# A split-fp32 decoder layer on one core: where the weights' low parts are made, which tile two copies use, and when the second half's sigmoids run

## The chip, the cores and the metric

One NeuronCore of a Trainium2 chip runs the kernel. The metric is the device time of one execution in microseconds (us); of the kernel before, three timed runs and one profiled execution are given. Its engines are TensorE (PE in the profile; PEld is its loading of weights), VectorE (DVE), ScalarE (ACT), GpSimd (POOL) and SyncE (SP), which here issues nearly all DMAs.

## The reference

One decoder layer on x of 2048 rows by 1024 columns, float32:

```python
xn = rms_norm(x, ln_g)
b, c, xc, gc, xl, gl = split(xn @ w_in)            # 6 parts of 1024 columns
y_conv = b * conv3(c * xc)                         # causal, depthwise
u = conv4(xl) + lru_conv_b
r, i = sigmoid(u @ w_a + b_a), sigmoid(u @ w_i + b_i)   # 16 heads of 64
a = exp(8 * r * log_sigmoid(lam))
h[t] = a[t] * h[t-1] + sqrt(1 - a[t]**2) * i[t] * u[t]
y = [headnorm(y_conv) * silu(gc), headnorm(h) * silu(gl)]
out = rms_norm(x + y @ w_out, final_g)
```

Two large products (1024 by 6144, and 2048 by 1024) make nearly all of the work on TensorE.

## The kernel before

**Products.** Each float32 operand is split into a high part (a cast to the matmul's float32r type, on ScalarE) and a low part (the operand minus the high part). A product is three matmuls: high with high, high with low, low with high (`mm`, line 924 of the profile). Seven products instead of eight per 2x2 block arrangement (Strassen's scheme in Winograd's form) are used, so sums of blocks are formed first (`add`) and results are added behind (`put`).

**Steps.** The work goes in steps of one block column. In the first half of the rows (h = 0) and in the second half (h = 1) three steps make a round: l (the LRU's input and its gate), a (two inputs of the short convolution) and b (its third input and its gate). Then come 16 steps o for the output projection. A step has seven slots; in each, twelve matmuls of 128x512 go into one PSUM bank. The order of the products is 0, 6 (of the step before), 1, 3, 2, 4, 5. Products 0, 1 and 2 of a step add up in one bank, called A; after each of them ScalarE copies the bank's state out: `q1` (line 1229) at slot 0, `u2` (line 1232) at slot 2, `rr` (line 1235) at slot 4. The next product into A may start only when the copy before it is done. `q1`, `u2` and `rr` have one tile each. `put(22)` reads rr in the same step; `put(21)` reads u2 at slot 1 of the next step, when product 6 is done (`pend`). Both are additions on VectorE (line 163, as all additions, subtractions and products of two tensors).

**Weights.** In the first half, `s_plan` splits the weights for step n+1 during step n and a little of n+1: `hi(i)` is the cast on ScalarE (line 200), `lo(i)` the subtraction. From step 4 to 23, lo(0), lo(4) and lo(6) run on GpSimd, the other four on VectorE. Each tile holds a high and a low part, and there are seven tiles in all (`sp`), so a cast must wait until PE has read the tile's last content and until its store has landed: the split weights are stored to DRAM (`sd`, line 205) two slots after the low part, or three where GpSimd made it. The second half loads them from there.

**What is due later.** `at(k, f)` puts f off by k slots and `tick()` runs what is due at the start of each slot; this sets the order of instructions on every engine. So the LRU's work runs over the two steps behind its own: the high and low parts of u (`sth`, `stl`; tile st) 5 and 6 slots after product 5, `gates(0)` (four matmuls into two gate banks, line 704) at 8, `sigs(0)` (their four sigmoids on ScalarE, line 711) at 9, `gates(1)` at 10 into the same two banks, `sigs(1)` at 11, then the decay, the scan and the rest up to 17. `silu` multiplies a gate by its sigmoid on GpSimd (tiles gl and gb).

Of the kernel before, what the change touches and what calls it, by code (L numbers as in the profile page):

```python
# [12 lines left out]
F32 = mybir.dt.float32  # L13
# [10 lines left out]
KT = D // P  # L24
# [14 lines left out]
def hymba_kernel(ctx: ExitStack, tc: tile.TileContext, x, xt, w_in, par, lamc, w_gate, w_out, final_g, out):  # L39
    nc = tc.nc  # L40
# [103 lines left out]
    def at(slots, *fs):  # L144
        if slots == 0:
            for f in fs:
                f()
        else:
            due.append([slots, fs])
# [20 lines left out]
    def low(v, hl, eng=None):  # L170
        tt(hl[1], v, hl[0].bitcast(F32), ALU.subtract, eng)
# [7 lines left out]
    def s_plan(n, r, dst):  # L179
        a11, a12, a21, a22 = r  # L180
        t, tiles = {}, {}

        def add(i):
            if i == 2:
                t[2] = aux("s1")
                tt(t[2], a21, a22, ALU.add)
            elif i == 1:
                t[1] = aux("s2")
                tt(t[1], t[2], a11, ALU.subtract)
            elif i == 3:  # L190
                tt(a21, a11, a21, ALU.subtract)
            else:
                tt(t[1], a12, t[1], ALU.subtract)

        def val(i):
            return {0: a11, 1: t.get(1), 2: t.get(2), 3: a21, 4: a12, 5: t.get(1), 6: a22}[i]

        def hi(i):
            tiles[i] = s_tile(dst, i)
            nc.scalar.copy(dst[i][0], val(i))  # L200

        def lo(i, eng=None):
            low(val(i), dst[i], eng)
            if PLAIN <= n < 3 * KT:
                at(3 if eng else 2, lambda: nc.sync.dma_start(sd[n][i], tiles[i].bitcast(F32)))

        g = nc.gpsimd if PLAIN < n < 3 * KT else None
        return [lambda: (add(2), add(1)),
                lambda: (hi(0), lo(0, g), add(3)),
                lambda: hi(1),  # L210
                lambda: (hi(3), lo(1)),
                lambda: (hi(2), lo(3), add(5)),
                lambda: (hi(4), lo(4, g), lo(2)),
                lambda: hi(5),
                lambda: (hi(6), lo(6, g), lo(5))]


    PLAIN = 3
# [18 lines left out]
    class TPrep:  # L237
# [12 lines left out]
        def lo(self, i, eng=None, v=None):  # L250
            low(self.val(i) if v is None else v, self.dst[i, self.j], eng)
# [410 lines left out]
    def lru(h, k, late=0):  # L662
# [33 lines left out]
        def gates(i):  # L696
            sl = slice(i * C, (i + 1) * C)
            if i == 0:
                v["r"], v["i"] = wt("r", "r"), wt("ig", "i", bufs=IG)
            v["ps"] = ps = []  # L700
            for j in range(2):
                ps.append(pss.tile([P, C], F32, tag="s", name="gate"))
                for n in range(2):
                    nc.tensor.matmul(ps[j], v["gw"][n][:, j, :], v["st"][j][:, sl],  # L704
                                     start=(n == 0), stop=(n == 1))

        def sigs(i):
            sl = slice(i * C, (i + 1) * C)
            for j, (hi, lo) in enumerate(((LO, HI), (HI, LO))):
                for g_, src, bias in ((v["r"], hi, BA), (v["i"], lo, BI)):  # L710
                    nc.scalar.activation(out=g_[hi, sl], in_=v["ps"][j][src], func=AF.Sigmoid,  # L711
                                         bias=pt[src, bias + k:bias + k + 1])
# [36 lines left out]
        def put(which, bank, other):  # L749
            dst = {11: o1[:, 4:4 + C], 12: o1[:, 4 + C:4 + N2], 21: g[:, 0:C], 22: g[:, C:N2]}[which]  # L750
            combine(dst, bank, other)
            if which == 12:
                at(1, c0)
                at(2, lambda: cj(1), lambda: cj(2), keep, gw)
                at(3, lambda: cj(3))
                for slots, *fs in ((5, sth), (6, stl), (8, lambda: gates(0)), (9, lambda: sigs(0)),
                                   (10, lambda: gates(1)), (11, lambda: sigs(1)), (12, s1, s0),
                                   (13, s1b), (14, s2, s3), (15, s4), (16, s5), (17, out_)):
                    at(slots + late, *fs)
            if which == 21:  # L760
                silu(g, late)
# [170 lines left out]
    def sm(tag):  # L932
        return small.tile([P, C], F32, tag=tag, name=tag)
# [29 lines left out]
    with tc.manual_schedule(engines={ENG.PE, ENG.Activation, ENG.DVE, ENG.Pool, ENG.SP}):  # L963
# [182 lines left out]
        for n in range(PLAIN, N):  # L1146
# [29 lines left out]
            for s in range(6 if late else 8 if new or last else 7):  # L1176
# [50 lines left out]
                if i == 0:  # L1227
                    q1 = sm("q1")
                    nc.scalar.copy(q1, bk["A"])  # L1229
                elif i == 1:  # L1230
                    u2 = sm_u2[0] = sm("u2")
                    nc.scalar.copy(u2, bk["A"])  # L1232
                elif i == 2:
                    rr = sm("rr")
                    nc.scalar.copy(rr, bk["A"])  # L1235
                    put(22, bk["B"], rr)
                    if late:
                        put(12, bk["D"], rr)
                elif i == 4:
                    put(11, bk["C"], q1)  # L1240
                elif i == 5 and not late:
                    put(12, bk["A"], None)
                elif i == 6:
                    put(21, bk["B"], u2)
# [50 lines left out]
```

## Time and profile before

| | us |
|---|---|
| median of three runs | 1357.18 (1356.16 to 1359.64) |
| the profiled execution | 1361.65 |
| its span | 1359.8 |
| PE / DVE / ACT / POOL busy | 1301.9 / 1032.5 / 748.4 / 226.2 |
| one round of the first half, steady | 60.70 |

The span is the time from the first to the last instruction of the profiled execution. In a row of the groups stand the line, engine, operation, the tile written and the tiles read (without numbers), the shape and count, then busy time in us, the mean of one in ns, and the engine's idle time just before these instructions with what ended it. In the timeline a row has start, duration, engine, line and operation, and in brackets an idle time ahead of it and who ended it. Matmul rows overlap, so PE's pace is read from their starts.

### The profile page before, as it was taken

What the parts mean: (1) busy time and instruction counts of PE and PEld (TensorE: products, weight loads), DVE (VectorE), ACT (ScalarE), POOL (GpSimd) and SP (SyncE); (2) the same over time, 40 slices, a digit from 0 to 9 for tenths busy, and PEclk for the clock granted to TensorE, in tenths of its full rate; (3) what the DMA queues carried; (4) which work ended last, traced back from release to release, by engine and by line L of the source; (5) the groups of instructions that cost most, each with busy time, mean ns of one, the idle gap of its engine ahead of it and who ended that gap; (6) DMA issues with size and microseconds to landing.
All of it is one profiled execution on the core that took longest, in us unless ns stands there. A gap on an engine that the chain in (4) does not pass through costs nothing.

```text
span 1359.8 us, 16618 instructions
## 1 busy us (share of the span) xinstructions
PE 1301.9 (96%) x5648; PEld 1058.6 (78%) x5648; DVE 1032.5 (76%) x1245; ACT 748.4 (55%) x1139; POOL 226.2 (17%) x160
## 2 busy tenths in 40 slices
PE   6989999999999999899999999999999799998997
PEld 5867877777878787777888888888878688887886
DVE  7778788789989897978566676667458776759885
ACT  7475757575665757565544645364456233444443
POOL 3204242333334340101010110101000000000000
PEclk9989999999999999999999999999999899999999
DMA  7137797988879888542789999999778889797643
GB/s 284 31 119 258 270 252 273 278 296 302 319 281 330 291 291 304 173 162 79 247 304 286 335 354 331 332 339 365 228 253 313 249 236 227 271 404 260 240 146 136
DMA packets 158805, 355.28 MB, mean 261 GB/s; under 512 B 17920, under 2 KB 52736, under 8 KB 158720
## 3 DMA queue, kind: packets, MB, share of 16 engines
q1 hardware_dynamic: 158432, 353.90, 77.1%
q8 instruction: 45, 0.74, 0.2%
q14 instruction: 40, 0.33, 0.1%
q10 hardware_dynamic: 288, 0.32, 0.1%
HBM read 217.11 MB, written 137.04 MB: 260 GB/s over the span
## 4 chain that ended last, share of the span: by engine, by line
PE 40%; DMA 7%; DVE 4%; ACT 3%; issue 1%; SPq 0%; DVEq 0%; ACTq 0%
PE bank L924 40%; DMA traw<-td 1%; DMA zr<-rsd 1%; PE gate L704 1%; ACT i L711 1%; ACT r L711 1%; DVE tl L163 1%; DMA traw<-in_w_out_dram 1%; DMA od<-xr 1%; DMA xr<-od 1%; DVE s L163 1%; DMA xr<-in_x_dram 1%; ACT th L435 1%; DMA yd<-gl 0%; DMA raw<-yd 0%
## 5 line engine op out<-in xcount | busy, mean ns | idle before, releaser
L924 PE MATMUL bank<-th,s 128*128 128x512 f32 x3632 | 1138.8, 392 | 19.9 <-ACT u L1232 10.0
L924 PEld LDWEIGHTS bank<-th,s 128*128 128x128 f32 x3632 | 686.1, 189 | 173.5 <-ACT u L1232 15.0
L924 PE MATMUL bank<-tl,s 128*128 128x512 f32 x1816 | 711.1, 392 | 1.6 <-DVE tl L163 1.3
L924 PEld LDWEIGHTS bank<-tl,s 128*128 128x128 f32 x1816 | 343.2, 189 | 74.8 <-DVE tl L163 3.5
L163 POOL TENSOR_TENSOR s<-raw,s 128x512 fp32r<-128x512 f32 x62 | 110.2, 1790 | 253.9 <-ACT s L200 210.7
L200 ACT CAST s<-raw 128x512 fp32r<-128x512 f32 x140 | 84.5, 616 | 75.4 <-PE bank L924 41.8
L163 DVE TENSOR_TENSOR tl<-traw,th 128x512 fp32r<-128x512 f32 x117 | 85.1, 763 | 40.4 <-ACT th L435 30.0
L1232 ACT COPY u<-bank 128x512 f32<-128x512 f32 x58 | 34.0, 586 | 145.6 <-PE bank L924 77.8
L163 DVE TENSOR_TENSOR s<-s,s 128x512 fp32r<-128x512 f32 x105 | 95.5, 909 | 10.5 <-ACT s L200 10.5
L163 POOL TENSOR_TENSOR gb<-gb,sg 128x1024 f32<-128x1024 f32 x16 | 40.6, 2537 | 348.3 <-ACT sg L637 328.2
L163 DVE TENSOR_TENSOR s<-raw,s 128x512 fp32r<-128x512 f32 (+1 forms) x125 | 92.7, 765 | 6.5 <-ACT s L982 4.4
L200 ACT CAST s<-s 128x512 fp32r<-128x512 f32 x105 | 64.7, 616 | 30.3 <-DVE s L163 25.8
L435 ACT CAST th<-traw 128x512 fp32r<-128x512 f32 x96 | 55.1, 618 | 30.7 <-DMA traw<-td 17.8
L1229 ACT COPY q<-bank 128x512 f32<-128x512 f32 x58 | 33.9, 584 | 68.0 <-PE bank L924 59.2
L678 DVE SCALAR_TENSOR_TENSOR u<-xl,pt,u 128x1024 f32<-128x1024 f32 x48 | 62.7, 1306 | 6.3 <-ACT u L674 5.7
L163 DVE TENSOR_TENSOR raw<-raw,zr 128x512 f32<-128x512 f32 x64 | 41.2, 684 | 34.6 <-DMA zr<-rsd 31.1
L1235 ACT COPY rr<-bank 128x512 f32<-128x512 f32 x58 | 33.8, 583 | 50.4 <-PE bank L924 50.4
L788 DVE SCALAR_TENSOR_TENSOR t<-p,pt,t 128x1024 f32<-128x1024 f32 x32 | 46.5, 1454 | 5.9 <-ACT t L785 5.1
L163 DVE TENSOR_TENSOR st<-u,st 64x1024 fp32r<-64x1024 f32 x32 | 46.5, 1452 | 1.0
L711 ACT ACTIVATE r<-gate,pt 64x512 f32<-64x512 f32 x64 | 43.8, 684 | 3.1 <-PE gate L704 2.4
L163 POOL TENSOR_TENSOR gl<-gl,sg 128x1024 f32<-128x1024 f32 x16 | 40.4, 2523 | 24.5 <-ACT sg L637 24.5
L711 ACT ACTIVATE i<-gate,pt 64x512 f32<-64x512 f32 x64 | 43.8, 684 | 1.1
(153 smaller groups left out, 1153.7 us busy)
## 6 DMA issues: line engine op xcount, KB each, us to landing
sd<-s SPq DMA_DIRECT2D x151, 512.0 KB
s<-sd SPq DMA_DIRECT2D x151, 512.0 KB
raw<-in_w_in_dram SPq DMA_DIRECT2D x104, 256.0 KB
raw<-yd SPq DMA_DIRECT2D x64, 256.0 KB
traw<-in_w_out_dram SPq DMA_DIRECT2D x64, 256.0 KB
so<-so SPq DMA_DIRECT2D x22, 512.0 KB
s<-so SPq DMA_DIRECT2D x22, 512.0 KB
yd<-gl SPq DMA_DIRECT2D x32, 256.0 KB
```

Source lines behind the costliest of these rows:

```text
L163: (eng or nc.vector).tensor_tensor(out=out, in0=a, in1=b, op=op)
L200: nc.scalar.copy(dst[i][0], val(i))
L435: nc.scalar.copy(self.dst[i, j][0], self.r[i, j])
L678: nc.vector.scalar_tensor_tensor(out=v["u"], in0=o1[:, 1 + j:1 + j + N2], scalar=lw[j], in1=v["u"], op0=ALU.mult, op1=ALU.add)
L704: nc.tensor.matmul(ps[j], v["gw"][n][:, j, :], v["st"][j][:, sl], start=(n == 0), stop=(n == 1))
L711: nc.scalar.activation(out=g_[hi, sl], in_=v["ps"][j][src], func=AF.Sigmoid, bias=pt[src, bias + k:bias + k + 1])
L788: nc.vector.scalar_tensor_tensor(out=tcur["t"], in0=p[:, 2 + j:2 + j + N2], scalar=cw[j], in1=tcur["t"], op0=ALU.mult, op1=ALU.add)
L924: nc.tensor.matmul(bank, a[:, js], b, start=start and n == 0, stop=stop and n == 2, skip_group_check=more)
L1229: nc.scalar.copy(q1, bk["A"])
L1232: nc.scalar.copy(u2, bk["A"])
L1235: nc.scalar.copy(rr, bk["A"])
```

## The change

Three edits. (1) `lo` loses its engine argument: VectorE makes all low parts of the first half, and the store of each follows two slots later. (2) u2 and rr use the tiles named u2 and rr in even steps, and each other's in odd steps. (3) For h = 1, sigs(0) and sigs(1) are due at 8 and 10, which are the slots of gates(0) and gates(1).

```diff
-        def lo(i, eng=None):
-            low(val(i), dst[i], eng)
+        def lo(i):
+            low(val(i), dst[i])
             if PLAIN <= n < 3 * KT:
-                at(3 if eng else 2, lambda: nc.sync.dma_start(sd[n][i], tiles[i].bitcast(F32)))
-
-        g = nc.gpsimd if PLAIN < n < 3 * KT else None
+                at(2, lambda: nc.sync.dma_start(sd[n][i], tiles[i].bitcast(F32)))
+
         return [lambda: (add(2), add(1)),
-                lambda: (hi(0), lo(0, g), add(3)),
+                lambda: (hi(0), lo(0), add(3)),
                 lambda: hi(1),
                 lambda: (hi(3), lo(1)),
                 lambda: (hi(2), lo(3), add(5)),
-                lambda: (hi(4), lo(4, g), lo(2)),
+                lambda: (hi(4), lo(4), lo(2)),
                 lambda: hi(5),
-                lambda: (hi(6), lo(6, g), lo(5))]
+                lambda: (hi(6), lo(6), lo(5))]
...
-                for slots, *fs in ((5, sth), (6, stl), (8, lambda: gates(0)), (9, lambda: sigs(0)),
-                                   (10, lambda: gates(1)), (11, lambda: sigs(1)), (12, s1, s0),
+                for slots, *fs in ((5, sth), (6, stl), (8, lambda: gates(0)), (9 - h, lambda: sigs(0)),
+                                   (10, lambda: gates(1)), (11 - h, lambda: sigs(1)), (12, s1, s0),
...
-                    u2 = sm_u2[0] = sm("u2")
+                    u2 = sm_u2[0] = sm(("u2", "rr")[n % 2])
...
-                    rr = sm("rr")
+                    rr = sm(("rr", "u2")[n % 2])
```

PE's order of instructions is the same before and after. On VectorE, in slots 1 to 3 of a step l of the first half, the kernel before has the following (s1, s2: sums of weight blocks; gb: a gate, which `put(21)` finishes from u2; s: a tile of split weights):

```order
L163 TENSOR_TENSOR s2_3095<-s1_3093,raw_2973 128x512
L163 TENSOR_TENSOR gb_2874<-bank_2981,u2_2961 128x512
L619 SCALAR_TENSOR_TENSOR gl_2546<-r_2878,pt_164,gl_2546 128x1024
L163 TENSOR_TENSOR s_3069<-s2_2912,s_3069 128x512
L163 TENSOR_TENSOR raw_2974<-raw_2973,raw_2974 128x512
```

The changed kernel has at the same place:

```order
L163 TENSOR_TENSOR s2_3096<-s1_3094,raw_2973 128x512
L163 TENSOR_TENSOR gb_2874<-bank_2981,u2_2961 128x512
L618 SCALAR_TENSOR_TENSOR gl_2546<-r_2878,pt_164,gl_2546 128x1024
L163 TENSOR_TENSOR s_3112<-raw_2789,s_3112 128x512
L163 TENSOR_TENSOR s_3069<-s2_2913,s_3069 128x512
L163 TENSOR_TENSOR s_3116<-raw_2973,s_3116 128x512
L163 TENSOR_TENSOR raw_2974<-raw_2973,raw_2974 128x512
```

The two rows that read raw_2789 and raw_2973 are lo(6) and the next step's lo(0); they came from GpSimd, and lo(0) stands ahead of the third sum (raw_2974).

On ScalarE, in slots 0 to 3 of a step b of the second half, the kernel before has (q1 and u2: the copies of bank A; r and i: the sigmoids; t: the convolution's first pass):

```order
L1229 COPY q1_6452<-bank_6439 128x512
L711 ACTIVATE r_6424<-gate_6426,pt_164 64x512
L711 ACTIVATE i_6425<-gate_6426,pt_164 64x512
L711 ACTIVATE r_6424<-gate_6429,pt_164 64x512
L711 ACTIVATE i_6425<-gate_6429,pt_164 64x512
L785 ACTIVATE t_6481<-p_6267,pt_164 128x1024
L1232 COPY u2_6499<-bank_6439 128x512
L711 ACTIVATE r_6424<-gate_6474,pt_164 64x512
```

The changed kernel has there (a cast of another job, so, stands between):

```order
L710 ACTIVATE r_6424<-gate_6426,pt_164 64x512
L710 ACTIVATE i_6425<-gate_6426,pt_164 64x512
L710 ACTIVATE r_6424<-gate_6429,pt_164 64x512
L710 ACTIVATE i_6425<-gate_6429,pt_164 64x512
L394 CAST so_6439<-s3_6337 128x512
L1228 COPY q1_6456<-bank_6443 128x512
L710 ACTIVATE r_6424<-gate_6474,pt_164 64x512
L710 ACTIVATE i_6425<-gate_6474,pt_164 64x512
L710 ACTIVATE r_6424<-gate_6477,pt_164 64x512
L710 ACTIVATE i_6425<-gate_6477,pt_164 64x512
L784 ACTIVATE t_6485<-p_6267,pt_164 128x1024
L1231 COPY rr_6503<-bank_6443 128x512
```

sigs(0) moved ahead of the q1 copy, sigs(1) ahead of t and of the u2 copy, which in this odd step writes the tile rr.

On SyncE, around the second of the two stores of rsx (512 single numbers, the row norms of the second half), the kernel before has (sd: stores of split weights; yd: of a finished gate):

```order
L624 DMA yd1_85<-gl_1519 128x4x128
L205 DMA sd9_103<-s_2036 128x1024
L539 DMA rsx1_91<-rs4_614 128x4x1
L205 DMA sd9_103<-s_2077 128x1024
L205 DMA sd10_104<-s_2081 128x1024
```

The changed kernel has:

```order
L623 DMA yd1_85<-gl_1519 128x4x128
L205 DMA sd9_103<-s_2077 128x1024
L205 DMA sd9_103<-s_2036 128x1024
L205 DMA sd10_104<-s_2081 128x1024
L538 DMA rsx1_91<-rs4_614 128x4x1
```

The stores of s_2077 (tile 6 of a step) and s_2081 (tile 0 of the next) moved from behind rsx to ahead of it.

## Prediction

> **What bounds the kernel now.** I read the page first, then PE's waits by stretch, then PE's own rows around a wait, and only then the engines that PE waits for.
>
> ```profile
> span 1359.8 us, 16618 instructions
> PE 1301.9 (96%) x5648; PEld 1058.6 (78%) x5648; DVE 1032.5 (76%) x1245; ACT 748.4 (55%) x1139; POOL 226.2 (17%) x160
> ```
>
> TensorE (PE) is busy for 96% of the span and the change leaves its instructions alone, so only time in which PE waits can be won or lost. Its waits from 84 to 540 us, where the first half's steady steps lie, and from 600 to 1030 us, the second half (columns: who waits for whom, us in total, times, longest):
>
> ```profile
> PE bank L924 <- ACT u L1232: 6.0, 8, 1.9
> PE bank L924 <- ACT q L1229: 4.0, 3, 2.5
> PE gate L704 <- DVE st L163: 2.2, 5, 1.1
> PE gate L704 <- ACT i L711: 1.2, 7, 0.2
> ...
> PE gate L704 <- ACT i L711: 2.0, 7, 0.3
> ```
>
> So PE waits for the copy of u2 (eight times), for the low parts of st (five times), and for the sigmoids before it may write the gate banks again. What one wait costs is read from PE's rows:
>
> ```profile
> 421.09 0.39 PE L924 MATMUL bank<-tl,s 128*128 128x512 f32 x1
> 421.31 0.39 PE L924 MATMUL bank<-th,s 128*128 128x512 f32 x1
> 422.11 0.50 PE L924 MATMUL bank<-th,s 128*128 128x512 f32 x1 [0.41 <-ACT u L1232]
> 422.45 0.39 PE L924 MATMUL bank<-tl,s 128*128 128x512 f32 x1
> ```
>
> Starts are 0.22 us apart (421.09, 421.31). Over the wait they are 0.80 and then 0.34 apart: 0.70 us lost for a wait of 0.41. The surcharge is 0.28 us a wait; I use it for all.
>
> A long wait also costs clock. The stages behind the two longest waits of the first half, and one whole round of three steps (l, a, b) in steady state:
>
> ```profile
> core 0: us, PE busy (x) PEld busy (x) DVE busy (x) ACT busy (x) POOL busy (x), PEclk, DMA share, GB/s
> 130.00:135.00 5.00, 4.93 (x15) 3.90 (x16) 3.08 (x4) 4.37 (x7) 4.33 (x4) 0.66 0.62 249
> 252.00:257.00 5.00, 4.53 (x13) 3.62 (x14) 3.48 (x4) 2.74 (x6) 2.46 (x3) 0.68 1.03 401
> 391.20:451.90 60.70, 59.86 (x262) 48.58 (x261) 56.36 (x58) 38.47 (x57) 23.23 (x15) 1.00 0.88 306
> ```
>
> At a granted clock of 0.66 and 0.68, about a third of 5 us is lost: 1.7 and 1.6 us. The round of 60.70 us runs at full clock.
>
> The rule for this in the Trainium skill (TensorE: Matmul & The Clock Gate, Part 1: The HAM clock gate) is that PE falls to half clock after an idle window of about 3.4 us. By it waits of 1.9 and 2.5 us would cost no clock, and the sum below would lose 2.5 us; the rows show the lower clock, so they decide.
>
> **Part 1: the copies swap tiles.** u2 of a step is read by VectorE (DVE) one step later, at slot 1 (put 21). Today the next u2 copy, at slot 2, writes the same tile and so waits for that read. ScalarE (ACT), 84 to 540 us, and one case of it on both engines:
>
> ```profile
> ACT u L1232 <- DVE gb L163: 27.5, 6, 4.7
> ACT u L1232 <- DVE gl L163: 19.5, 5, 5.9
> ...
> 420.70 0.68 DVE L163 TENSOR_TENSOR gb<-bank,u 128x512 f32<-128x512 f32 x1
> 421.47 0.59 ACT L1232 COPY u<-bank 128x512 f32<-128x512 f32 x1 [4.55 <-DVE gb L163]
> ```
>
> After the swap the copy writes the tile that held rr, last read at slot 4 of the step before, five slots earlier. DVE's lag no longer reaches the copy, and PE at slot 4 (the third product into bank A) finds it done: here it could run 4.55 us sooner, and PE waited only 0.41. The new reader-before-writer is rr: its copy at slot 4 now follows put(21) at slot 1 of the same step, three slots earlier (a slot is twelve products, 12 x 0.226 = 2.7 us).
>
> Worth: 6.0 + 8 x 0.28 = 8.2 us; I take off one wait (0.7) for a copy that is late for other work, and add the clock behind the wait of 1.9 us, 1.7. That is 9.2 us, with ends 4 (see the first rival) and 9.9. Next in line at this place is the rr copy, two slots on.
>
> **Part 2: the lows on DVE.** 60 subtractions (three a step, nine a round) leave GpSimd (POOL). Here is what POOL pays, and DVE beside it, in the round 330.5 to 391.2 us; below the dots the same groups from 700 to 760 us, where POOL makes no lows:
>
> ```profile
> L163 POOL TENSOR_TENSOR s<-raw,s 128x512 fp32r<-128x512 f32 x9 | 16.5, 1849 | 30.0 <-ACT s L200 30.0
> ...
> L163 DVE TENSOR_TENSOR s<-s,s 128x512 fp32r<-128x512 f32 x9 | 9.7, 1078 | 0.5 <-ACT s L200 0.5
> L163 DVE TENSOR_TENSOR s<-raw 128x512 f32<-128x512 f32 x3 | 4.2, 1412 | 0.0
> L163 DVE TENSOR_TENSOR s<-s,raw 128x512 f32<-128x512 f32 x3 | 3.0, 1016 | 0.1
> L163 DVE TENSOR_TENSOR u<-T,u 128x1024 f32<-128x1024 f32 x1 | 2.1, 2147 | 0.0
> L788 DVE SCALAR_TENSOR_TENSOR t<-p,pt,t 128x1024 f32<-128x1024 f32 x2 | 3.5, 1740 | 0.0
> ...
> L163 DVE TENSOR_TENSOR s<-raw 128x512 f32<-128x512 f32 x1 | 0.7, 666 | 0.0
> L163 DVE TENSOR_TENSOR u<-T,u 128x1024 f32<-128x1024 f32 x1 | 1.2, 1219 | 0.0
> L788 DVE SCALAR_TENSOR_TENSOR t<-p,pt,t 128x1024 f32<-128x1024 f32 x2 | 2.6, 1284 | 0.0
> ```
>
> The same DVE operations run longer where POOL runs: with 0.67 us as the floor of a 128x512 one, 9 x 0.41 + 3 x 0.74 + 3 x 0.35 + 0.93 + 2 x 0.46 = 8.8 us a round. Some of it belongs to POOL's two gate products, which stay:
>
> ```profile
> 364.25 2.50 DVE L163 TENSOR_TENSOR s<-s,s 128x512 fp32r<-128x512 f32 x1 [0.53 <-ACT s L200]
> ...
> 382.97 2.44 DVE L163 TENSOR_TENSOR s<-s,s 128x512 fp32r<-128x512 f32 x1
> ```
>
> They are 1.8 us each over the floor, so 3.6 stay and 5.2 go. In exchange DVE gets nine operations at 0.61 apart (336.46 and 337.07 in the rows below): 5.5 us. DVE's load per round stays as it is, 56.4 of 60.70 us, within half a microsecond. What changes is where it lies: of the 5.2 us, about 1 us each went at three places just ahead of the waits that PE feels (the sum s<-raw and the st pair among them), while the added operations may run anywhere in the time before PE reads them: a low made at slot 2 or 6 is read five slots, 13 us, later at the earliest.
>
> The new wait is DVE's for the cast of the same slot: low 0, 4 and 6 stand right behind their own cast in the code, so DVE's queue holds until ACT has cast. Where that bites is slot 2 of step b:
>
> ```profile
> 336.46 0.68 DVE L163 TENSOR_TENSOR s<-s,s 128x512 fp32r<-128x512 f32 x1
> 337.07 0.69 DVE L163 TENSOR_TENSOR raw<-raw 128x512 f32<-128x512 f32 x1
> ...
> 337.72 1.13 ACT L200 CAST s<-raw 128x512 fp32r<-128x512 f32 x2
> ```
>
> DVE comes there at 336.46, the first cast ends near 338.3: 1.8 us idle, with the convolution (t) and the LRU's u queued behind, whose results PE does not want for ten slots. I cost it at nothing; DVE's idle time of 60.70 - 56.36 = 4.3 us a round covers it.
>
> The five st waits: the pair runs late and is itself stretched,
>
> ```profile
> 386.04 3.46 DVE L163 TENSOR_TENSOR st<-u,st 64x1024 fp32r<-64x1024 f32 x2
> ```
>
> against 2 x 1.2 without POOL, so the second ends 1.0 us sooner even if nothing before it moves; the typical wait is a quarter of that. They are worth at most 2.2 + 5 x 0.28 = 3.6; I take 3.0, because the longest (1.1 us) may stay in part. Ends 0 and 3.6.
>
> **Part 3: the sigmoids a slot sooner, second half.** sigs(0) now stands at the slot of gates(0) and not behind the q1 copy of that slot; gates(1), two slots on, finds its banks read. The four sigmoids of 0.7 us fit in the slot in which they now start. Worth 2.0 + 7 x 0.28 = 4.0 us, ends 3 and 4. The first half keeps its seven waits. At slot 2 the u2 copy now stands behind sigs(1) and the convolution's first pass; with 2.8 + 1.2 us of work in a slot of 2.7 it may come a microsecond late, and PE wants it two slots on.
>
> **Part 4: the stores move.** The stores of lows 0, 4 and 6 go out one slot sooner on SP's queue. One place matters. The q wait of 2.5 us:
>
> ```profile
> 237.62 0.49 SPq L205 DMA_DIRECT2D sd<-s  x1
> 238.20 0.61 SPq L539 DMA_DIRECT2D rsx<-rs  x1
> ...
> 245.00:250.00 5.00, 5.00 (x23) 3.80 (x21) 4.96 (x7) 1.43 (x2) 0.00 (x0) 1.00 0.37 9
> ...
> 251.31 0.62 ACT L200 CAST s<-s 128x512 fp32r<-128x512 f32 x1 [4.28 <-DMA sd<-s]
> ```
>
> Behind the store of rsx (512 single numbers) the DMA moves 9 GB/s for 5 us; the sd store issued just ahead of it lands late, ACT's cast into that tile waits 4.28 us, and q behind it. In the new order another store stands between that one and rsx, so the tile wanted first should be free in time; but the store next to rsx is now another tile's, wanted two slots later. The wait is worth 2.5 + 0.28 + 1.6 (clock) = 4.4; ends 0 and 4.4, and I take the middle, 2.2.
>
> **Sum.** 9.2 + 3.0 + 4.0 + 2.2 = 18.4 us. The profiled execution took 1361.65 us, 1.85 of it outside the span; it would take 1343.3. It lies 4.5 us above the median of the three runs, 1357.18, so the same sum puts the median at 1338.8 us.
>
> **Rivals.**
>
> *The waits move on (about 9 us gained).* In ACT's queue the silu's sigmoid follows the u2 copy and still waits for the same DVE result (put 21); behind it come the casts and rr, which PE wants two slots after u2. Where DVE lags by over three slots PE then waits for rr. For it: waits for u of 4.55 and 5.9 us are two slots long. Against it: rr has 5.4 us more time than u2 had. Half of parts 1 and 2 and nothing of part 4 would be left with part 3: 4.6 + 1.5 + 4.0, rounded down to 9, 1348 us.
>
> *Nothing that can be measured.* All of it turns up at the next wait of the same slot. Runs of this kernel can be told apart by 0.3%, 4.1 us: 1353 to 1361 us. Against it: in the first half's list of waits rr does not appear at all, and the round has 4.3 us of idle DVE.
>
> *Slower: DVE becomes the bound.* If the long DVE operations do not shorten, a round needs 56.4 + 5.5 + 1.8 (the wait for casts) = 63.7 us of DVE where PE needs 60.70: 3.0 us more a round, over (540 - 84) / 60.7 = 7.5 rounds 22 us; less part 3, 18: 1375 us. It decides from the point at which less than 3.0 us a round comes back; the rows say 5.2, which is why it has little chance.
>
> The Trainium skill speaks for this rival (Perfetto Trace Analysis, Optimizing Scalar/DVE Operations): when VectorE is saturated, giving work to ScalarE or GpSimd may pay, and this change does the reverse; its next sentence says that between GpSimd and VectorE it might not help since they share a port, which is what the stretched rows show.
>
> **How the numbers follow.** The forecast has 0.68, the moved waits 0.17, nothing 0.08, slower 0.07. Faster by over 0.3% is 0.68 + 0.17 = 0.85. The forecast's own range is 1335 (all upper ends: 9.9 + 3.6 + 4.0 + 4.4 = 21.9) to 1346 (11; all lower ends at once would be 7). Taking in the first rival's 1348 with a microsecond to spare gives 1334 to 1349.
>
> **What would show it.** Right: waits of PE for u (L1231 after the change) from 84 to 540 us under 1.5 us in total, those for st under 0.6, those for i in the second half gone, the round near 59.5 us, s<-raw and u<-T,u at 0.7 and 1.2 us in the round. Wrong: DVE over 58 us in a round of over 60.7, new waits of PE for rr, or DVE lows in PE's list of waits.

## The result: 8.9 us faster, and where TensorE stops now

| | us |
|---|---|
| before, median of four runs | 1358.41 (1356.16 to 1359.81) |
| after, median of four runs | 1349.48 (1348.44 to 1351.38) |
| ratio | 0.9936, 95% interval 0.9919 to 0.9953 |
| profiled execution: before, after | 1361.65, 1350.12 |

The changed kernel is faster by 0.64% (interval 0.47% to 0.81%), half of the 18.4 us that the prediction had. First the page of the profile after:

```profile
span 1348.3 us, 16504 instructions
PE 1296.9 (96%) x5648; PEld 1060.1 (79%) x5648; DVE 1032.5 (77%) x1305; ACT 749.5 (56%) x1139; POOL 124.1 (9%) x100
```

GpSimd (POOL) has 60 instructions fewer, VectorE (DVE) 60 more, and DVE is busy for as long as before, 1032.5 us. The sixty lows have cost DVE nothing in sum. PE's waits from 84 to 540 us, the same stretch as in the prediction:

```profile
PE bank L923 <- ACT rr L1234: 3.5, 2, 2.1
PE bank L923 <- ACT q L1228: 2.9, 2, 1.6
PE gate L703 <- DVE st L163: 1.6, 3, 0.6
PE bank L923 <- ACT u L1234: 1.4, 1, 1.4
PE gate L703 <- ACT i L710: 1.2, 7, 0.2
PE bank L923 <- ACT rr L1231: 0.4, 1, 0.4
```

The name of a tile has to be read with its line, since the change swaps names: line 1231 is the copy of slot 2 (u2 before), line 1234 the copy of slot 4 (rr before). The eight waits for the copy of slot 2 are down to one of 0.4 us. In their place PE waits for the copy of slot 4, as `rr` and as `u`, 4.9 us, which did not appear at all before. In the second half, 600 to 1020 us, PE waits for nothing, and the i waits (2.0 us, seven times) are gone.

One steady round (columns as in the prediction):

```profile
332.00:391.87 59.87, 59.64 (x262) 48.63 (x261) 55.45 (x66) 38.57 (x57) 7.34 (x6) 1.00 0.86 308
```

The round takes 59.87 us against 60.70; the prediction said 59.5. What the missing part is can be read from the rows of that round. On DVE, around the third sum of the weights (`raw<-raw`):

```profile
356.36 0.68 DVE L163 TENSOR_TENSOR gb<-bank,u 128x512 f32<-128x512 f32 x1
...
359.36 2.89 DVE L163 TENSOR_TENSOR s<-raw,s 128x512 fp32r<-128x512 f32 x1
362.18 0.68 DVE L163 TENSOR_TENSOR raw<-raw 128x512 f32<-128x512 f32 x1
```

On GpSimd at that time, the silu's gate product:

```profile
359.01 2.69 POOL L163 TENSOR_TENSOR gb<-gb,sg 128x1024 f32<-128x1024 f32 x1 [17.14 <-ACT sg L636]
```

On ScalarE (ACT):

```profile
357.87 1.06 ACT L636 ACTIVATE sg<-gb 128x1024 f32<-128x1024 f32 x1
...
362.93 0.62 ACT L200 CAST s<-raw 128x512 fp32r<-128x512 f32 x1 [2.53 <-issue]
363.46 0.58 ACT L1234 COPY u<-bank 128x512 f32<-128x512 f32 x1
```

And on PE:

```profile
363.65 0.94 PE L923 MATMUL bank<-th,s 128*128 128x512 f32 x2
364.44 0.40 PE L923 MATMUL bank<-tl,s 128*128 128x512 f32 x1
```

Read it backwards. From 363.65 two matmuls take 0.79 us to the next start, where two at full pace take 0.45: PE lost 0.34 us for the slot-4 copy, which ended at 364.04. The copy stood behind a cast of the third sum, which began at 362.93, right after the sum (362.18 + 0.68 = 362.86); the profile names no releaser there, the times do. The sum came late because the low ahead of it took 2.89 us and not 0.69, and it took that long while GpSimd's product ran (359.01 to 361.70). The product could start then because its sigmoid follows the slot-2 copy and a table load of 1.28 us on ACT, and these no longer wait for DVE's put(21) (gb at 356.36). The sigmoid itself still reads what put(21) writes: it starts 0.83 us behind its end, where it was 1.99 us in the kernel before (gb at 359.98, sigmoid at 362.65). In that kernel the product held back lows at 364.25 and 382.97 (2.50 and 2.44 us, shown in the prediction), which nobody needed soon.

In a steady round PE loses only 0.3 us by this. Most of the loss is three long waits for the slot-4 copy, at 137, 181 and 243 us, and they are made in the same way. The rows of the second, on four engines:

```profile
174.81 2.89 POOL L163 TENSOR_TENSOR gb<-gb,sg 128x1024 f32<-128x1024 f32 x1 [17.98 <-ACT sg L636]
175.34 2.90 DVE L163 TENSOR_TENSOR s<-s,s 128x512 fp32r<-128x512 f32 x1
...
178.77 0.68 DVE L163 TENSOR_TENSOR raw<-raw 128x512 f32<-128x512 f32 x1
...
180.05 0.58 ACT L1234 COPY rr<-bank 128x512 f32<-128x512 f32 x1
180.68 0.50 PE L923 MATMUL bank<-th,s 128*128 128x512 f32 x1 [1.45 <-ACT rr L1234]
```

Between the third sum and the copy stands its cast again, at 179.53. At 137 us the product held the third sum itself (2.87 us from 132.78).

The rule that bears on this in the Trainium skill (SBUF — State Buffer, Who interferes with whom) says that a VectorE instruction with two inputs in SBUF contends with a GpSimd instruction that reads SBUF, through a shared read port. The trace agrees: 2.89 against 0.69 us.

For a count over whole kernels I take PE's starts: what lies beyond 0.227 us from one matmul to the next, where it is over 0.06 us, summed in three stretches. They are cut at the same matmuls in every kernel, those that start at 100, 560 and 1020 us in the kernel before (first half, second half, and the rest). Each row is one profiled execution:

| kernel | first half | second half | rest | median, ratio to before |
|---|---|---|---|---|
| before | 24.2 | 12.1 | 16.4 | 1 |
| after | 19.4 | 6.2 | 15.4 | 1349.48, 0.9936 |
| lows alone | 17.0 | 11.5 | 21.6 | 1358.12, 0.999 |
| swap alone | 20.0 | 11.8 | 21.6 | 1356.95, 0.9986 |
| sigmoids alone | 19.6 | 7.8 | 15.8 | 1352.83, 0.9955 |
| after, third sum early | 17.0 | 6.0 | 15.4 | 1347.72, 0.992 |
| after, slot-4 copy first | 21.1 | 5.9 | 17.0 | 1353.37, 0.9958 |
| after, gate product on DVE | 8.9 | 6.2 | 16.8 | 1338.77, 0.9844 |
| before, gate product on DVE | 15.2 | 11.3 | 18.5 | 1353.89, 0.997 |
| after, silu two slots later | 21.1 | 6.5 | 17.0 | 1350.88, 0.9946 |
| product on DVE, lows on GpSimd | 9.2 | 6.3 | 18.0 | 1341.16, 0.9879 |
| product on DVE, third sum early | 10.0 | 6.1 | 19.3 | 1343.61, 0.9879 |
| product on DVE, all sigmoids sooner | 5.7 | 4.4 | 18.8 | 1335.77, 0.9832 |
| all of these | 5.2 | 4.4 | 16.1 | 1334.54, 0.9817 |

Two pairs of these numbers show how much a single profile is worth. The sigmoids alone leave the first half's code as it was, and it loses 19.6 us there against 24.2. The lows alone leave the last stretch as it was, and it loses 21.6 us there against 16.4. So a difference of 5 us between two rows shows nothing by itself; verdicts below come from the ratios, each made against runs of the kernel before of the same session, and the traces are used for the place.

### The profile page after: what moved, and what is told of

It is laid out like the page before. It is cut to its first block, busy times and chain, and to the rows that moved or that the text cites. A ratio compares the mean times of both kernels' runs of the same rounds, so it can differ in the third digit from the quotient of the medians.

```text
span 1348.3 us, 16504 instructions
## 1 busy us (share of the span) xinstructions
PE 1296.9 (96%) x5648; PEld 1060.1 (79%) x5648; DVE 1032.5 (77%) x1305; ACT 749.5 (56%) x1139; POOL 124.1 (9%) x100
## 4 chain that ended last, share of the span: by engine, by line
PE 70%; DMA 9%; DVE 8%; ACT 2%; issue 2%; SPq 0%; POOL 0%; DVEq 0%; POOLq 0%; ACTq 0%
PE bank L923 69%; DMA traw<-td 2%; DVE tl L163 2%; PE gate L703 2%; DMA bd<-in_w_gate_dram 2%; DMA zr<-rsd 1%; DVE s L163 1%; ACT i L710 1%; ACT r L710 1%; DVE traw L163 1%; DMA traw<-in_w_out_dram 1%; DMA sd<-s 1%; DMA s<-sd 1%; DMA xr<-od 1%; DMA od<-xr 1%
## 5 line engine op out<-in xcount | busy, mean ns | idle before, releaser
L163 DVE TENSOR_TENSOR s<-raw,s 128x512 fp32r<-128x512 f32 (+1 forms) x185 | 140.4, 774 | 26.4 <-ACT s L200 16.3
L163 POOL TENSOR_TENSOR gb<-gb,sg 128x1024 f32<-128x1024 f32 x16 | 43.3, 2708 | 462.8 <-ACT sg L636 427.0
L163 DVE TENSOR_TENSOR s<-s,s 128x512 fp32r<-128x512 f32 x105 | 78.7, 749 | 0.8 <-ACT s L200 0.8
L787 DVE SCALAR_TENSOR_TENSOR t<-p,pt,t 128x1024 f32<-128x1024 f32 x32 | 41.0, 1283 | 14.6 <-ACT t L784 14.0
L1231 ACT COPY rr<-bank 128x512 f32<-128x512 f32 x31 | 18.1, 585 | 51.3 <-PE bank L923 51.3
L163 DVE TENSOR_TENSOR traw<-traw 128x512 f32<-128x512 f32 x60 | 43.9, 733 | 1.9 <-DMA traw<-in_w_out_dram 0.7
L1231 ACT COPY u<-bank 128x512 f32<-128x512 f32 x27 | 15.8, 585 | 52.5 <-PE bank L923 52.4
L163 DVE TENSOR_TENSOR st<-u,st 64x1024 fp32r<-64x1024 f32 x32 | 42.3, 1322 | 1.0
```

The source lines that it names most:

```text
L163: (eng or nc.vector).tensor_tensor(out=out, in0=a, in1=b, op=op)
L787: nc.vector.scalar_tensor_tensor(out=tcur["t"], in0=p[:, 2 + j:2 + j + N2], scalar=cw[j], in1=tcur["t"], op0=ALU.mult, op1=ALU.add)
```

## The experiments

**The three edits alone.** The theory drawn from the traces at this point (called T in the expectations): with the swap, PE's stop moves from the slot-2 copy to the slot-4 copy, because the lows now stand ahead of the third sum. Its rival: the stop has another cause than the lows.

Lows on VectorE, u2 and rr and the sigmoids as before (left out below: `lo` without its engine argument, and its store after two slots, as in the change):

```diff
-                lambda: (hi(0), lo(0, g), add(3)),
+                lambda: (hi(0), lo(0), add(3)),
...
-                lambda: (hi(4), lo(4, g), lo(2)),
+                lambda: (hi(4), lo(4), lo(2)),
...
-                lambda: (hi(6), lo(6, g), lo(5))]
+                lambda: (hi(6), lo(6), lo(5))]
```

> Theory T: in the changed kernel PE's new waits for rr come from the lows that now stand ahead of the third sum (raw<-raw) on VectorE; the cast of that sum is late and the rr copy queues behind it on ScalarE. Rival A: the rr copy is late because the silu's sigmoid ahead of it waits for put(21). Rival B: it is late because after the swap rr writes the tile that put(21) reads. This kernel has the lows on VectorE and nothing else, so u2 and rr keep their own tiles. T: waits of 1.4 us or more for rr stay near 137, 180 and 243 us, and the steady round still waits a little for rr; with part of the u waits left, the gain is 2 to 5 us. B: no wait for rr at all, gain 6 us or more. A: as T.

Measured: 1358.12 us, ratio 0.999 (0.9973 to 1.0007): nothing that can be told from none, where T had 2 to 5 us and B 6 or more. Its steady round is 59.5 us all the same. In the table its first half loses 7.2 us less than the kernel before and its last stretch 5.2 us more; whether a gain is hidden there stays open. PE's waits from 84 to 540 us:

```profile
PE gate L703 <- DVE st L163: 3.1, 4, 1.6
PE bank L923 <- ACT q L1228: 3.0, 2, 1.7
PE bank L923 <- ACT u L1231: 2.0, 4, 0.6
PE bank L923 <- ACT rr L1234: 1.3, 1, 1.3
```

The u waits fell from 6.0 to 2.0 us with the swap left out. One wait for rr is there without the swap, so B is out; T had three. In this kernel the slot-2 copy still waits for put(21), and the sigmoid behind it with it. Around the third sum on DVE:

```profile
355.38 0.69 DVE L163 TENSOR_TENSOR gb<-bank,u 128x512 f32<-128x512 f32 x1
...
358.98 0.69 DVE L163 TENSOR_TENSOR raw<-raw 128x512 f32<-128x512 f32 x1
359.58 2.90 DVE L546 SCALAR_TENSOR_TENSOR xcol<-xcol,pt 128x512 f32<-128x512 f32 x1
```

and on GpSimd:

```profile
359.20 2.73 POOL L163 TENSOR_TENSOR gb<-gb,sg 128x1024 f32<-128x1024 f32 x1 [18.30 <-ACT sg L636]
```

Counted from the start of gb, the product starts 3.82 us later, with the swap 2.65. Here it meets an instruction behind the sum, there one ahead of it. That is the first sign that the lows as such are not what holds the slot-4 copy.

The swap alone:

```diff
-                    u2 = sm_u2[0] = sm("u2")
+                    u2 = sm_u2[0] = sm(("u2", "rr")[n % 2])
...
-                    rr = sm("rr")
+                    rr = sm(("rr", "u2")[n % 2])
```

> The tiles swapped and nothing else; the three lows stay on GpSimd, the sigmoids where they were. T: the u waits of 6.0 us from 84 to 540 us go and the third sum stands where it stood, so the waits for rr are shorter than the changed kernel's 3.9 us (rr and u at line 1235 together); gain 5 to 9 us. Rivals A and B: the waits for rr are as long as the changed kernel's or longer, since VectorE lags more with GpSimd beside it; gain 2 to 5 us.

Measured: 1356.95 us, ratio 0.9986 (0.9974 to 0.9998), 1.9 us and at most 3.5, where T had 5 to 9 and its rivals 2 to 5. The waits for the slot-2 copy (line 1232) are down to 0.6 us here as well, and others have come:

```profile
PE gate L704 <- DVE st L163: 4.8, 8, 1.5
...
PE bank L924 <- ACT rr L1235: 1.2, 2, 0.7
```

The waits for the slot-4 copy are 1.9 us (rr and u), shorter than the changed kernel's 4.9, as T said; but st waits went from 2.2 us (five) to 4.8 (eight). On DVE the product, which starts at 358.25, meets the third sum itself, with no low added ahead of it:

```profile
358.79 2.88 DVE L163 TENSOR_TENSOR raw<-raw 128x512 f32<-128x512 f32 x1
```

So the swap does what it says, and alone it is worth almost nothing.

The sigmoids alone:

```diff
-                for slots, *fs in ((5, sth), (6, stl), (8, lambda: gates(0)), (9, lambda: sigs(0)),
-                                   (10, lambda: gates(1)), (11, lambda: sigs(1)), (12, s1, s0),
+                for slots, *fs in ((5, sth), (6, stl), (8, lambda: gates(0)), (9 - h, lambda: sigs(0)),
+                                   (10, lambda: gates(1)), (11 - h, lambda: sigs(1)), (12, s1, s0),
```

> The kernel before with the third edit alone: the second half's sigmoids a slot sooner. Both theories say the same here, since the first half is untouched: the waits of PE for the second half's i tiles (some 4 us in 600 to 1020 us in the kernel before) are gone, nothing takes their place, and the kernel is 3 to 5 us faster than before (ratio 0.996 to 0.998). If the ratio is 0.999 or more, the gain seen in the second half of the changed kernel needs the first half's edits, which none of the theories says.

Measured: ratio 0.9955 (0.9941 to 0.9969), 6.1 us, interval 4.2 to 8.0. PE's lost time in the second half falls by 12.1 - 7.8 = 4.3 us in the table, near the forecast of 4.0; what the median has beyond that can't be placed, since the code of the other stretches is the same. PE waits for no sigmoid in the second half. This is the one edit that pays by itself, two thirds of the whole gain.

**The way to the slot-4 copy.** Third sum ahead of the lows, in the changed kernel:

```diff
-        return [lambda: (add(2), add(1)),
-                lambda: (hi(0), lo(0), add(3)),
+        return [lambda: (add(2), add(1), add(3)),
+                lambda: (hi(0), lo(0)),
```

> The changed kernel with the third sum formed with the first two, one slot sooner, ahead of put(21) and of the lows. T: the waits for rr of 2.1, 1.4 and 1.4 us near 137, 180 and 243 us and the small ones of the steady rounds go, 3.9 us of waiting and about 1.7 us of clock with their surcharges: 5 to 8 us faster than the changed kernel, 1341 to 1344 us on the scale of the earlier runs. A and B: put(21) comes 0.6 us later, so the waits for rr stay or grow; no faster than the changed kernel.

Measured: 1347.72 us, ratio 0.992 (0.9904 to 0.9936), 1.8 us below the changed kernel, where T had 5 to 8. PE's waits from 84 to 540 us:

```profile
PE gate L703 <- DVE st L163: 5.2, 6, 1.7
PE bank L923 <- ACT q L1228: 3.5, 2, 2.2
PE bank L923 <- ACT rr L1231: 1.6, 2, 1.2
```

No wait for line 1234 is left, so the sum is what its cast, and behind it the copy, had waited for. The st waits grew by 3.6 us instead, and the kernel is not to be told from the changed one.

The slot-4 copy ahead of that cast (the split's fourth group, with hi(3), issued behind the copy):

```diff
-                elif s > 0:
+                elif s > 0 and (late or s != 4):
                     prep(n + 1, s - 1)
...
                     if late:
                         put(12, bk["D"], rr)
+                    if not late and not new:
+                        prep(n + 1, s - 1)
```

> The changed kernel with the cast of the third sum (and the low beside it) put behind the rr copy of the same slot; VectorE's order of lows and third sum stays. T: rr no longer stands behind that cast, so the waits for rr from 84 to 540 us fall from 4.9 us (rr and u there) to under 1; 4 to 7 us faster than the changed kernel. A and B: the sigmoid and the tile are as before, the waits for rr stay at 3 us or more, same time within 2 us.

Measured: 1353.37 us, ratio 0.9958 (0.9943 to 0.9972), 5.6 us slower than the run above and 3.9 above the changed kernel, where T had 4 to 7 below it. The waits for line 1234 are gone here too, and st takes it all:

```profile
PE gate L703 <- DVE st L163: 6.8, 10, 2.2
```

Both edits take away the wait that the traces showed and win little or nothing. The theory that the order of the lows and the sum sets the time is not enough; something holds DVE, and PE feels it at whichever place is next.

**The gate product.** From here on there are three theories: A, the product on GpSimd holds the instruction ahead of the third sum, since the swap lets it start sooner; B, the number of lows ahead of the sum; C, whatever wait goes, the next one takes its place. In the changed kernel the first half's product goes to VectorE (left out here and below: `silu` is handed h, the half):

```diff
-        at(4 + late, lambda: tt(g, g, sg[0], ALU.mult, nc.gpsimd))
+        at(4 + late, lambda: tt(g, g, sg[0], ALU.mult, nc.gpsimd if h else None))
```

> The changed kernel with the silu's gate product of the first half on VectorE in place of GpSimd, nothing else moved. Theory A (in the changed kernel GpSimd's gate product of 2.7 us starts with the sooner sigmoid and holds the VectorE low ahead of the third sum to 2.9 us; the rr copy of slot 6 stands behind that sum's cast): the low takes 0.7 us again, the rr copy's waits of slot 6 (7.6 us over the profile's 84 to 540 us) fall under 2 us, the round goes from 59.9 to 59.5 us or less, the whole 4 to 8 us faster than the changed kernel. Theory B (the number of lows ahead of the sum holds it, not the collision): the rr waits stay above 5 us, and the product adds 0.7 to 1.3 us to VectorE in each step: same as the changed kernel or 1 to 3 us slower. Theory C (whatever wait goes, the next one takes its place): rr waits go, st or q waits grow by as much, time within 2 us of the changed kernel.

Measured: 1338.77 us (1337.04 to 1340.05), ratio 0.9844 (0.9825 to 0.9863), 10.7 us below the changed kernel by the medians and 12.5 by the ratios; A had 4 to 8. PE's waits from 84 to 540 us and a steady round:

```profile
PE gate L703 <- DVE st L163: 1.7, 4, 0.6
PE bank L923 <- ACT q L1228: 1.3, 1, 1.3
PE gate L703 <- ACT i L710: 1.1, 7, 0.2
PE bank L923 <- ACT rr L1231: 0.4, 1, 0.4
PE bank L923 <- ACT u L1231: 0.2, 1, 0.2
```

```profile
332.00:391.50 59.50, 59.34 (x262) 48.73 (x261) 53.47 (x69) 38.88 (x57) 1.84 (x4) 1.00 0.89 315
```

The waits for line 1234 are gone and nothing has come for them. (They were 4.9 us in the changed kernel, at slot 4; the expectation's 7.6 us and slot 6 are in no list of waits.) DVE does two products more in the round and is busy for less, 53.47 against 55.45 us: a product costs it 1.2 us of its own and had cost it 2.2 in a held instruction. At the place of the rows above, the low and the sum now read:

```profile
349.83 0.69 DVE L163 TENSOR_TENSOR s<-raw,s 128x512 fp32r<-128x512 f32 x1
350.43 0.69 DVE L163 TENSOR_TENSOR raw<-raw 128x512 f32<-128x512 f32 x1
```

B and C are out: the number of lows is the same, and the next wait did not come. C was right only as long as the product stayed on GpSimd.

Is it the product's place, or the product on GpSimd wherever it lies (A')? The same line in the kernel before, with none of the three edits:

> The kernel before, with the silu's gate product of the first half on VectorE and nothing else. Theory A (the product on GpSimd costs 8 to 11 us in the changed kernel because the swap lets it start sooner, ahead of the third sum): the kernel before gains less than half of that here, 0 to 4 us; its waits for u stay above 4 us, since they come from VectorE's lag at put 21. Theory A' (the product on GpSimd costs VectorE time wherever it lies, and any lag of VectorE reaches PE by some way): the kernel before gains as much as the changed one did, 8 to 11 us, with the waits for u falling under 2 us. Theory B (the number of lows): gains 0 to 2 us.

Measured: 1353.89 us, ratio 0.997 (0.9954 to 0.9986), 4.1 us, interval 1.9 to 6.2. The waits of PE:

```profile
PE bank L924 <- ACT u L1232: 5.7, 8, 1.5
PE bank L924 <- ACT q L1229: 3.0, 2, 1.7
...
```

The u waits stay (5.7 us, 6.0 before), as A said, and the st waits are gone. 4.1 us lies at A's upper end. With the product on DVE the three edits together take the ratio from 0.997 to 0.9844: 1.26%, 17 us (15 by the medians, 12 by the profiled executions), where with the product on GpSimd they take it to 0.9936.

The product left on GpSimd, the silu two slots later in the changed kernel, behind the slot-4 copy:

```diff
-        at(2 + late, f1)
-        at(4 + late, lambda: tt(g, g, sg[0], ALU.mult, nc.gpsimd))
+        at(2 + late if h else 4 + late, f1)
+        at(4 + late if h else 6 + late, lambda: tt(g, g, sg[0], ALU.mult, nc.gpsimd))
```

> The changed kernel with the silu's sigmoid and product of the first half two slots later, the product still on GpSimd: the sigmoid then stands behind the rr copy on ScalarE. Theory A (the place of the product): the rr copy's waits of slot 6 go from 7.6 us (with what stands behind them in the list, PE's waits for rr and u of line 1234) to under 2 us, 3 to 8 us faster than the changed kernel. Theory A' (its load on VectorE wherever it lies): the rr waits go, but st, q or gl waits of the same size come, time within 2 us of the changed kernel. Theory B: the rr waits stay, same time.

Measured: 1350.88 us, ratio 0.9946 (0.9929 to 0.9962), no faster than the changed kernel. The largest of PE's waits:

```profile
PE gate L703 <- DVE st L163: 8.7, 9, 2.5
```

The waits for line 1234 went, as A and A' said, and the time did not, as A' alone said. The rows show why. On DVE, the pair of st lows, 2 x 1.22 us in the changed kernel:

```profile
321.74 4.65 DVE L163 TENSOR_TENSOR st<-u,st 64x1024 fp32r<-64x1024 f32 x2
```

and on GpSimd:

```profile
321.65 2.40 POOL L163 TENSOR_TENSOR gl<-gl,sg 128x1024 f32<-128x1024 f32 x1 [3.43 <-ACT sg L636]
```

The product meets the st pair now, and PE waits for st. So each theory has a half: wherever it lies, the product holds the DVE instruction that it meets until it has ended (A'); whether PE feels it depends on which one that is (A). In the steady rounds of the kernel before it met lows without a near reader.

**What the lows are worth once the product is off GpSimd**, and the best order. Lows 0, 4 and 6 back on GpSimd in the kernel with the product on DVE (the first edit undone):

> The changed kernel with the gate product of the first half on VectorE, but with lows 0, 4 and 6 back on GpSimd with their stores a slot later: edits 2 and 3 and the product. It tells what the first edit is worth once the product is off GpSimd. Forecast's term: 3.0 us for st and up to 4.4 for the place of the rsx store, so 3 to 7 us slower than the run with the product alone. Theory A': GpSimd's lows of 1.85 us then hold VectorE as the product did, st and rr waits of 3 us or more return, 4 to 8 us slower. Theory C (the first edit is worth nothing, as it was alone): within 1.5 us of 1338.8.

Measured: 1341.16 us, ratio 0.9879 (0.9856 to 0.9902): slower by 2.4 us by the medians, by 0.35% or 4.8 us by the ratios, which come from two sessions. PE's waits are 0.8 us for st and 0.6 for the two copies, not the 3 us or more of A', and the first half loses 9.2 us against 8.9. So what the lows are worth is not settled. The swap's worth can be read from the table: from the kernel before with the product on DVE to this one, where only the swap changes the first half, it falls from 15.2 to 9.2 us. This is 6.0 us from two single profiles, and the swap was not run alone with the product on DVE.

The third sum early, with the product on DVE (the two edits shown above):

> The changed kernel with both: the third sum ahead of the lows, and the gate product on VectorE. Theory A: with the third sum early the rr waits are gone already (they were in the run with that alone, 1.8 us faster than the changed kernel); the product's place then decides only the st waits (5.2 us there): they fall under 2.5 us, and the whole is 2 to 4 us faster than the run with the third sum alone. Theory B: the product adds load on VectorE, st waits stay at 5 us or grow; within 1 us of that run or slower. Theory C: as B.

Measured: 1343.61 us, ratio 0.9879 (0.9861 to 0.9897), 4.1 us faster than with the early sum alone, near the 2 to 4 of A, and 4.8 us slower than with the product alone. The st waits fell from 5.2 to 1.2 us, so the product had made those too. The table has 1.1 us of the 4.8 in the first half and 2.5 in the last stretch, where the code is the same. Why it is slower stays open.

All of it, with the first half's sigmoids a slot sooner too:

```diff
-                for slots, *fs in ((5, sth), (6, stl), (8, lambda: gates(0)), (9 - h, lambda: sigs(0)),
-                                   (10, lambda: gates(1)), (11 - h, lambda: sigs(1)), (12, s1, s0),
+                for slots, *fs in ((5, sth), (6, stl), (8, lambda: gates(0)), (8, lambda: sigs(0)),
+                                   (10, lambda: gates(1)), (10, lambda: sigs(1)), (12, s1, s0),
```

> As the run before it, and the first half's sigmoids a slot sooner as well. Theory A: the i waits of the first half go too (0.2 us in each step, some 1.3 us in 84 to 540 us): 1 to 3 us faster than the run before it. Theory C: the sooner sigmoid stands ahead of a cast or copy on ScalarE, and a wait for st, rr or u of the same size comes in its place: no difference above 1 us, or slower.

Measured: 1334.54 us (1332.81 to 1338.01), ratio 0.9817 (0.9795 to 0.9839): 9 us below the run before it, where 1 to 3 were expected; PE waits for no sigmoid in the first half.

The same without the early sum:

> The changed kernel with the gate product of the first half on VectorE and the first half's sigmoids a slot sooner too, the third sum left in its place. All theories that hold the i waits for real: seven of 0.2 us with their surcharge of 0.28, so 3 us faster than the run with the product alone (1338.8), near 1335. If the early third sum was what cost 4.8 us between the two runs with the product on VectorE, this is the fastest of all, 1331 to 1336; if that was chance of the build, it is level with the run of everything (1334.5).

Measured: 1335.77 us, ratio 0.9832 (0.9805 to 0.9859). PE's waits from 84 to 540 us:

```profile
PE bank L923 <- ACT q L1228: 2.0, 1, 2.0
PE gate L703 <- DVE st L163: 1.1, 2, 0.5
...
```

The two can't be told apart, so with the sooner sigmoids the place of the third sum made no difference; that it cost 4.8 us without them may be chance of the build, which no run settles. The two are 1.7 and 1.8% faster than the kernel before, and 14 to 15 us below the changed kernel: the fastest found.

## Why the prediction failed in the first half

- **Where it stands.** Part 3 was right and a little small. For the first half the prediction had 9.2 + 3.0 + 2.2 = 14.4 us; the table has 24.2 - 19.4 = 4.8. The miss lies there. Comparing the distance from each matmul to the next in both profiled executions, clock included, places it: part 1 is worth 0.9 us, st of part 2 0.9, and the q waits of part 4 3.0.
- **Part 1 is the step that failed**: its term of 9.2 us, by the sentence "rr has 5.4 us more time than u2 had", with which the rival of the moved waits was put at 0.17. The waits for the slot-2 copy did go, and their end is worth 9.3 us; the new waits for line 1234, two slots on, which the prediction had named as a sign of being wrong, take back 8.4. Alone the swap is worth 0.14%. The time that rr had was counted from put(21), whereas rr stood behind a cast of the third sum, and the part named neither that cast nor the sum, nor the product that now starts sooner and holds the sum or a low ahead of it for 2.2 us.
- **Part 2: the load was right, the freedom of the added operations was not.** DVE's round fell from 56.36 to 55.45 us where I had it stay, s<-raw and u<-T,u are at 0.7 and 1.2 us. But the added operations were said to "run anywhere in the time before PE reads them": I asked only when PE reads a low, and not what stands behind it on DVE: two of them stand ahead of the third sum. The st term of 3.0 us came to 0.9: the steady rounds' waits went, and three others of 1.6 us in all stayed or came, where under 0.6 was forecast. The row in which GpSimd's two products were counted ("they are 1.8 us each over the floor, so 3.6 stay") priced them as load of a constant size; their place was what changed.
- **The first rival is what happened**, with 0.17: PE waits for rr, and 1349.48 us lies near its 1348. It had the right chain of casts and the right copy, but took DVE's lag at put(21) for the cause. The sigmoid does wait for put(21), yet it came sooner behind it than before, and its product did the harm. The nearness of the number is luck: its sum left 4.6 us of part 1 and nothing of part 4, where 0.9 and 3.0 came.
- **Part 3**: waits for i in the second half gone; 4.3 us by the traces of the sigmoids alone, 6.1 (4.2 to 8.0) by its runs, against 4.0. The u2 copy behind sigs(1) cost nothing.
- **Part 4**: the q wait of 2.5 us at 252 us is gone in the changed kernel, which with its clock is the upper end, 4.4; a q wait at 124 us grew and takes back 1.3. But in the kernel with the sigmoids alone, where no store has moved, the wait at that place was 1.4 us and cost no clock. Part of this gain is chance; the stores' move was not tried alone.
- **The clock terms** (1.7 us in part 1, 1.6 in part 4) were taken as a price that goes with the wait. They are chance, as the last section shows: in the kernel with the sigmoids alone the very same wait of 1.9 us is there and cost none. The profiled execution of before lies 3.2 us above its median, so about 3 us of the 18.4 were hardly to be had.
- **The slower rival** did not come: 56.36 + 5.5 - 55.45 = 6.4 us of DVE came back in a round, where 5.2 were counted on and 3.0 were needed.
- **The forecast's number** was that of a kernel without the product on GpSimd: 1338.77 measured, 59.50 us a round. Its 4.1 us from the product's own move are in that. What the three edits are worth there, 12 to 17 us as said above, is the fair comparison with 18.4. By the table 15.2 - 8.9 = 6.3 us of it lie in the first half, where the forecast had 14.4, so the agreement is in good part luck.

## What to carry to other kernels

When a wait is taken away, follow what its waiting engine now does sooner, down to the instructions of other engines that this starts, and look at what they will run beside. An instruction is urgent if it is read soon or if anything queued behind it on its engine is; list the queue up to the next value that the bound engine reads. And where edits win little, try them together with the suspected common cause removed: here 12 to 17 us came of edits that showed 9.

## What the runs showed of the hardware

- **A VectorE instruction with two inputs in SBUF that starts while a GpSimd product runs ends a fixed time after the product.** In the traces of all runs 226 such instructions start inside a gate product. All but two end 0.55 to 0.57 us after it where they are 128x512 (0.69 us long undisturbed), and 1.08 to 1.15 us after it where they are 1024 wide (1.22 undisturbed): the instruction stands until the product has ended and then takes nearly its own time. So 0.69 us became 2.87 to 2.90 beside products of 2.69 to 2.89 us, and of the st pair of 4.65 the first took 3.39 beside a product of 2.40, the second its usual time. The 50 additions that read a PSUM bank (`xx<-bank,u`) and start inside a product all take 0.69 us, and reductions with one input stay at 1.25.
- **The same wait costs clock in one execution and none in the next.** At the change from the first half to the second PE waits for q in all kernels, 2.9 us in most of them. PE's row there and the 5 us behind it, in the kernel with the third sum early:

```profile
561.83 0.50 PE L923 MATMUL bank<-th,s 128*128 128x512 f32 x1 [2.87 <-ACT q L1228]
```

```profile
561.90:566.90 5.00, 5.00 (x22) 4.16 (x23) 5.00 (x5) 3.60 (x7) 3.32 (x2) 1.00 0.92 328
```

and in the one with the lows alone:

```profile
562.51 0.79 PE L923 MATMUL bank<-th,s 128*128 128x512 f32 x1 [2.87 <-ACT q L1228]
```

```profile
562.60:567.60 5.00, 5.00 (x12) 3.94 (x13) 5.00 (x4) 3.08 (x6) 3.84 (x3) 0.50 0.72 292
```

A wait of 2.87 us each time, in two kernels, and then 22 matmuls in 5 us at a granted clock of 1.00, or 12 at 0.50. In the kernel with the sigmoids alone the wait of 1.9 us that cost 1.7 us of clock in the prediction's rows is there too, at full clock:

```profile
129.86 0.50 PE L924 MATMUL bank<-th,s 128*128 128x512 f32 x1 [1.90 <-ACT u L1232]
```

```profile
129.80:134.80 5.00, 4.94 (x22) 4.07 (x23) 3.44 (x5) 4.96 (x8) 4.33 (x4) 1.00 0.63 250
```

The Trainium skill (TensorE: Matmul & The Clock Gate, Part 1: The HAM clock gate) says that the activity window runs freely, and that the point at which the clock changes depends on where in the window the work falls. That fits these pairs; its length of 3.4 us for an idle window, by which no wait shown here could cost clock, does not. A clock seen behind a short wait is an estimate's upper end, not its middle.
- **The turn to the output projection differs from kernel to kernel** where the code is the same: PE's wait there was 4.8 us in the kernel with the sigmoids alone and 8.8 in the one with the lows alone. PE waits there for the tile rt of DVE, which in its queue stands behind waits for a reload from DRAM (`zr<-rsd`): 0.68 us just ahead of it in the first kernel, 6.47 and 1.44 in the second. What sets that landing wasn't tried.
